# Order of the high-part and low-part products inside a weight unit of a two-block transformer kernel

## Chip, cores and metric

The kernel runs on one core of one Trainium2 chip. The metric is the device time of one execution in microseconds (us); a comparison is made by the median of several runs.

## Reference

Two transformer blocks over 256 tokens of width 2048 in float32. The first block has a mixer (a gated delta rule with eight heads beside a short convolution), an attention over 256 memory rows and a feed-forward layer with 5632 hidden features; the second has two kinds of causal attention with output gates. Nearly all arithmetic is products of 256 tokens with weight matrices:

```python
h = rmsnorm(x, mix_norm[l])
proj = h @ w_mix_in[l]
...
x = x + jnp.concatenate([y_gdn, y_sc], axis=-1) @ w_mix_out[l]
...
x = x + memory_xattn(h, mem_n, w_q[l], w_k[l], w_v[l], w_o[l])
x = x + conv_ffn(h, w_ffn_up[l], ffn_conv[l], w_ffn_down[l])
```

## Kernel before

**Products in parts.** Weights and operands are split into a high part (rounded to the float32r format that TensorE takes) and a low part, the exact remainder. A product is high times high, plus high weights times low operand, plus low weights times high operand. The moving operand of a K-tile, class `XT`, is one tile of 128 partitions by 512 columns: 256 columns of high part beside 256 of low part (`x.t`, with `x.hi` and `x.lo` its halves).

**Weight units.** The weights come in 704 units. A unit of `jobB` holds up to eight blocks of 128 x 128 weights for one tile of 128 output features, and a tile takes two units (three for some of `w_xo`). `blocks` (lines 207 to 224) issues a unit's products. Where `wide` is set, one matmul of 512 columns (line 217) multiplies the high weights with both halves of the operand, and one of 256 columns (line 222) the low weights with the high half. Otherwise there are two matmuls of 256 columns with the high weights (lines 219 and 220) and one with the low weights (line 222). The order is all high products of the unit, then all low products; in the last unit of a wide tile the last high product (line 224) comes at the very end, since it closes both halves of the bank. Every matmul has a weight load of its own. `jobA` (lines 306 to 308, 84 units) has the weights as moving operand and is not touched.

**Splitting and loading.** `stream` issues the work unit by unit. Ahead of unit i it issues `split_hi(i + 3)` (ScalarE copies the raw weights into a tile `whi`, line 352, four buffers) and `split_lo(i + 2)` (VectorE subtracts to make a tile `wlo`, line 359, three buffers), and the DMA load of a later unit through SyncE's queue, eight raw buffers deep. Then come the unit's products, and one step of every running piece of side work (norms, convolutions, softmax, the delta rule), whose instructions stand in the same queues of VectorE, ScalarE and GpSimd. Each engine runs its queue in the order in which it was written.

**Start.** `first_x` makes the first sixteen operand tiles: ScalarE the high part, VectorE the low part (line 537). In VectorE's queue the split of unit 0 stands behind operand tile 3, that of unit 1 behind tile 7, and those of the units from 2 on behind tile 15. The first three units belong to three different output tiles and all use operand tiles 0 to 7.

Of the kernel before, what the change touches and what calls it, by code (L numbers as in the profile page):

```python
# [15 lines left out]
PSUM = bass.MemoryType.PSUM  # L16
# [11 lines left out]
# columns of the packed per-partition parameters  # L28
# [11 lines left out]
# square constants: identity, ones, upper triangle, causal bias (negated), levels of the inverse,  # L40
# identities of 16 x 16 flattened
# [12 lines left out]
class XT(Ev):  # L54
    """One K-tile of a product's moving operand: [128, 256] as exact hi and lo parts."""
# [12 lines left out]
class Half:  # L68
    """[128, 256] float32 tiles, two to a slab."""
# [30 lines left out]
def block_rows(d):  # L100
    """Four 128 x 128 matrices in DRAM, spaced so that all their diagonal blocks lie evenly."""
    return bass.AP(tensor=d.tensor, offset=0, ap=[[P, P], [P * P + P, 4], [1, P]])
# [6 lines left out]
class Builder:  # L109
# [18 lines left out]
    # ---- storage  # L128
# [30 lines left out]
    # ---- side work: generators that go one step per weight unit  # L159
# [29 lines left out]
    # ---- the stream of weight units  # L189
# [17 lines left out]
    def blocks(self, ps, hi, lo, j0, xs, k0, n, first, last, wide):  # L207
        """128 x 128 blocks of weights, the high parts first. Wide: the high part's products with both
        parts of the operand lie side by side in the bank."""
        T, x = self.T, []  # L210
        c = [slice((j0 + j) * P, (j0 + j + 1) * P) for j in range(n)]
        end = n - 1 if wide and last else n
        for j in range(n):
            x.append(xs[k0 + j])
            self.need(x[j])
            if wide and j < end:
                T.matmul(ps, hi[:, c[j]], x[j].t, start=first and j == 0, stop=False)  # L217
            elif not wide:
                T.matmul(ps, hi[:, c[j]], x[j].hi, start=first and j == 0, stop=False)  # L219
                T.matmul(ps, hi[:, c[j]], x[j].lo, start=False, stop=False)  # L220
        for j in range(n):
            T.matmul(ps[:, 0:TOK], lo[:, c[j]], x[j].hi, start=False, stop=last and j == n - 1 and not wide)  # L222
        if end < n:
            T.matmul(ps, hi[:, c[end]], x[end].t, start=first and end == 0, stop=True)  # L224

    def merge(self, ps, out):
        """The two halves of a product's bank, added."""
        t = self.H("mg")
        self.AC.copy(t, ps[:, TOK:])  # L229
        yield  # L230
        self.V.tensor_tensor(out, ps[:, 0:TOK], t, ADD)
        self.rel()

    def times(self, ps, out, R):
        """A product's bank times a factor per token, once that is there. out: the tile, or a generator
        that gets it."""
        wide = ps.shape[1] > TOK
        if wide:
            t = self.H("ms")
            yield from self.merge(ps, t)  # L240
            while not R.ok:
                yield
            ps = t
        dst = out
        if not isinstance(out, bass.AP):
            dst = yield from out
        self.V.tensor_tensor(dst, ps, R.b, MUL)
        if not wide:
            self.rel()
        return dst  # L250

    def scaled_pre(self, ps, R):
        """The same into a tile with zeros before the first token."""
        pre = []

        def get():
            pre.append((yield from self.pre()))
            return pre[0][:, 4:]

        yield from self.times(ps, get(), R)  # L260
        return pre[0]

    def jobB(self, w, ui, parts, xs, post, ready=(), wide=False, srcs=None):
        """Features out on the partitions. parts: the K-tiles in each unit; post(ps) a generator."""
        st, units, k0 = {}, [], 0
        if wide:
            ready = ()
        K = sum(parts)
        for i, nk in enumerate(parts):
            def mm(hi, lo, k0=k0, nk=nk):  # L270
                if k0 == 0:
                    st["ps"] = self.mmbank()[:, 0 : (2 if wide else 1) * TOK]
                self.blocks(st["ps"], hi, lo, 0, xs, k0, nk, k0 == 0, k0 + nk == K, wide)

            last = i == len(parts) - 1
            pf = (lambda: [(ready, post(st["ps"]))]) if last else None
            src = self.A[w][ui + i] if srcs is None else srcs[i]
            units.append(self.unit(src, nk * P, mm, pf))
            k0 += nk
        return units  # L280

    def jobB_pair(self, w, ui, nk, xs, posts, ready=()):
        """Two column tiles in one unit."""
# [10 lines left out]
    def jobA(self, w, ui, K, xs, post, ready=(), early=None):  # L294
        """Tokens out on the partitions, 512 columns; two K-tiles to a unit. early(ps): the first half of
        the tokens is done first, and this follows it."""
# [32 lines left out]
    @staticmethod  # L329
    def skew(jobs, m):  # L330
        """The first units of the first m jobs before their second units."""
        out = []
        for i in range(max(len(j) for j in jobs[:m])):
            for j in jobs[:m]:
                if i < len(j):
                    out.append(j[i])
        for j in jobs[m:]:
            out += j
        return out
# [42 lines left out]
    # ---- small pieces  # L382
# [4 lines left out]
    def rsq(self, v, w):  # L387
        """v ** -0.5 for columns, with a Newton step."""
# [9 lines left out]
    def split_tile(self, src):  # L398
        """A slab's exact hi and lo parts."""
# [5 lines left out]
    def mm3(self, ps, a, b, first, last):  # L405
        """A product of two operands in hi and lo parts."""
# [4 lines left out]
    def sums(self, accs):  # L411
        """Column sums over the partitions of [128, 256] tiles, or of lists of them:
        [128 tokens, 2 for each]."""
# [12 lines left out]
    def spread(self, cols, n):  # L426
        """Columns [128 tokens, n] as rows over all partitions, in PSUM [128, n * 128]."""
# [12 lines left out]
    def g_rms(self, R, acc, width):  # L440
        """R: .c the factor per token [128, 2], .b the same over the partitions [128, 256]."""
# [13 lines left out]
    def prep(self, src, gain, x, acc, first):  # L455
        """The moving operand of a product after a norm whose factor per token comes later."""
# [11 lines left out]
    def conv(self, pre, taps, K):  # L468
        """Causal taps along the tokens; the tile holds 4 zeros before the first token."""
# [10 lines left out]
    # ---- constants and the first operand  # L480
# [22 lines left out]
    def first_x(self):  # L503
# [6 lines left out]
        # the tensor engine's clock is up to speed when the first operands are there  # L510
# [49 lines left out]
    # ---- mixer: decays and gates  # L560
    def softplus(self, z, w):
        """max(z, 0) + log1p(exp(-|z|)); the low part of 1 + y is carried along."""
# [97 lines left out]
    def g_gdn(self, g, t, done, base):  # L660
        """Four heads, 128 tokens: one chunk of the delta rule."""
# [213 lines left out]
    def g_base(self, base):  # L875
        """Inverses of the unit lower 16 x 16 diagonal blocks, one block to a partition."""
# [42 lines left out]
    # ---- mixer: short convolution  # L919
# [33 lines left out]
    # ---- memory  # L953
# [72 lines left out]
    # ---- residual stream  # L1026
# [14 lines left out]
    # ---- attention over the memory  # L1041
# [65 lines left out]
    # ---- feed-forward  # L1107
# [53 lines left out]
    def g_two_norms(self):  # L1161
        """The final norm of the first block and the first of the second."""
# [24 lines left out]
    def g_turn(self):  # L1187
        """The residual stream with the tokens on the partitions: 32 x 32 blocks turned by the vector
        engine, then put in their places on the way through DRAM."""
# [25 lines left out]
    # ---- second block: latents, rotary tables  # L1215
# [57 lines left out]
    def rope(self, r, out, rows):  # L1273
        """Rows in pairs of 32: x * cos + swapped x * sin, the sign in the sines."""
# [13 lines left out]
    def p_rf(self, ps):  # L1288
        """Rotary keys (rows 0-63) and forget gates (rows 64-71)."""
# [43 lines left out]
    # ---- causal attention of one head; keys 0-127 for the first queries, all for the others  # L1333
# [110 lines left out]
    def p_last(self, n):  # L1444
        """Tokens on the partitions: the last norm's factor is a column."""
# [20 lines left out]
    def g_out(self, ps, t):  # L1466
        """The last columns of half the tokens, the norm, the sum and the store."""
# [17 lines left out]
    def order(gd, zz, sc):  # L1485
        """The heads' tiles between others whose results take less work."""
        return gd[0:12] + zz[0:4] + sc[0:6] + gd[12:24] + zz[4:8] + sc[6:]

    # ---- the whole
    def build(self):  # L1490
# [12 lines left out]
        # streams are lists of units; hooks run before a unit's products  # L1503
# [5 lines left out]
        class Lazy(dict):  # L1509
            """K-tiles made by earlier work."""  # L1510
# [18 lines left out]
        # mixer  # L1529
# [4 lines left out]
        # tiles of w_mix_in: q 0-7, k 8-15, v 16-23, z 24-31, ba 32, then b, c, h of the convolution  # L1534
# [17 lines left out]
        # keys and values of the memory  # L1552
# [7 lines left out]
        # mixer out  # L1560
# [30 lines left out]
        # attention over the memory  # L1591
# [9 lines left out]
        for n in range(16):  # L1601
            # the last head's tiles in units of their own while it is still at work
# [6 lines left out]
        # feed-forward  # L1609
# [33 lines left out]
        # second block  # L1643
# [13 lines left out]
        # tiles of w_in_2: q_lat 0-5, kv_lat 6-9, rope and forget 10, gates of the first 11-18, fq 19-26,  # L1657
        # fk 27-34, gates of the second 35-42; fv apart
# [69 lines left out]
        # run  # L1728
# [25 lines left out]
# ---- host side: layout only  # L1754
# [4 lines left out]
def _b(w):  # L1759
    """[K, N] -> units of (up to 8 K-tiles) x 128 columns, K on the partitions."""  # L1760
# [8 lines left out]
def _a(w):  # L1769
    """[K, N] -> units of 2 K-tiles x 512 columns."""  # L1770
# [94 lines left out]
```

## Time and profile before

| what | value |
|---|---|
| median of 3 runs | 2087.55 us (2086.34 to 2087.66) |
| the profiled execution, first to last instruction | 2085.8 us |
| TensorE matmul busy, instructions | 2068.1 us (99%), 12526 |
| TensorE weight load busy, instructions | 1843.3 us (88%), 12526 |
| VectorE busy | 1463.8 us (70%) |
| ScalarE busy | 1081.7 us (52%) |
| DMA | 381.52 MB, mean 183 GB/s |

The profile has the span of the profiled execution; what lies around it in a run is 1.75 us by the median (2087.55 less 2085.8). Busy time of matmuls is the time in which at least one is under way; they overlap, so the length of one is more than its share, and the distance from one start to the next is what a product takes. PE stands for TensorE's matmuls, PEld for its weight loads, DVE for VectorE, ACT for ScalarE.

### The profile page before, as it was taken

To read this page: it belongs to the slowest core of one execution; us is meant where nothing else is said; L and a number is where in the kernel's file an instruction comes from. 1 tells how busy PE (TensorE), PEld (TensorE's weight loads), DVE (VectorE), ACT (ScalarE), POOL (GpSimd) and SP (SyncE) were. 2 spreads that over 40 slices of the span, in tenths; PEclk is the share of its full clock that TensorE was granted. 3 is DMA by queue.
4 is the path that set the end of the run, shared out by engine and by line. 5 is a ranking of instruction groups with operands and counts; after the bars stand their busy time and mean duration, and the time that the engine had idled before them with its cause. 6 is when DMAs were issued, how large, how long until landed. Compare 5 with 4: busy or idle time off the path is not lost.

```text
span 2085.8 us, 32625 instructions
## 1 busy us (share of the span) xinstructions
PE 2068.1 (99%) x12526; PEld 1843.3 (88%) x12526; DVE 1463.8 (70%) x2303; ACT 1081.7 (52%) x1701; POOL 186.7 (9%) x170
## 2 busy tenths in 40 slices
PE   8999999999999999999999999999999999999998
PEld 7999999988888898888888888888888889878886
DVE  7977668665467667688775778657779776557755
ACT  5654455544444555465543555435556644446653
POOL 3020012200001001100000000000009410000000
PEclk9999999999999999999999999999999999999999
DMA  7555446445565435555555555555546578444552
GB/s 279 172 163 183 152 142 225 162 162 191 193 228 187 161 118 190 191 189 188 186 194 182 192 192 188 186 192 188 186 152 220 200 220 222 161 143 152 196 186 102
DMA packets 136669, 381.52 MB, mean 183 GB/s; under 512 B 33601, under 2 KB 41537, under 8 KB 136513
## 3 DMA queue, kind: packets, MB, share of 16 engines
q1 hardware_dynamic: 136512, 379.44, 53.8%
q8 instruction: 98, 1.61, 0.3%
q14 instruction: 59, 0.48, 0.1%
HBM read 372.84 MB, written 5.90 MB: 182 GB/s over the span
## 4 chain that ended last, share of the span: by engine, by line
PE 98%; DVE 1%; DMA 0%; issue 0%; ACT 0%; SPq 0%; DVEq 0%
PE mm L217 42%; PE mm L222 28%; PE mm L219 5%; PE mm L220 5%; PE mm L306 4%; PE mm L308 4%; PE mm L307 4%; PE mm L224 3%; PE ps L1405 0%; PE ps L409 0%; PE ps L407 0%; PE ps L408 0%; PE ps L1404 0%; PE ps L781 0%; PE ps L764 0%; PE ps L1386 0%
## 5 line engine op out<-in xcount | busy, mean ns | idle before, releaser
L359 DVE TENSOR_TENSOR wlo<-raw,whi 128x1024 fp32r<-128x1024 f32 (+2 forms) x704 | 857.6, 1221 | 379.7 <-PE mm L222 133.6
L217 PE MATMUL mm<-x,whi 128*128 128x512 f32 x3786 | 965.1, 394 | 6.2 <-DVE x L537 5.7
L352 ACT CAST whi<-raw 128x1024 fp32r<-128x1024 f32 (+2 forms) x704 | 716.3, 1028 | 318.6 <-PE mm L308 106.6
L217 PEld LDWEIGHTS mm<-x,whi 128*128 128x128 f32 x3786 | 694.6, 189 | 138.1 <-DVE x L537 7.7
L222 PEld LDWEIGHTS mm<-x,wlo 128*128 128x128 f32 x4840 | 657.4, 191 | 41.4
L222 PE MATMUL mm<-x,wlo 128*128 128x256 f32 x4840 | 679.3, 283 | 0.0
L229 ACT COPY mg<-mm 128x256 f32<-128x256 f32 x182 | 67.8, 372 | 374.1 <-PE mm L224 373.9
L219 PE MATMUL mm<-x,whi 128*128 128x256 f32 x792 | 196.4, 285 | 0.0
L220 PE MATMUL mm<-x,whi 128*128 128x256 f32 x792 | 194.3, 283 | 0.0
L220 PEld LDWEIGHTS mm<-x,whi 128*128 128x128 f32 x792 | 151.5, 191 | 0.3
L219 PEld LDWEIGHTS mm<-x,whi 128*128 128x128 f32 x792 | 151.4, 191 | 0.2
L476 DVE SCALAR_TENSOR_TENSOR cv<-pre,cst,cv 128x256 f32<-128x256 f32 x264 | 130.5, 496 | 8.8 <-ACT cv L473 0.9
L306 PE MATMUL mm<-whi,x 128*128 128x512 f32 x336 | 131.9, 393 | 0.0
L308 PE MATMUL mm<-whi,x 128*128 128x512 f32 x336 | 130.9, 390 | 0.0
L307 PE MATMUL mm<-wlo,x 128*128 128x512 f32 x336 | 130.8, 389 | 0.0
L224 PE MATMUL mm<-x,whi 128*128 128x512 f32 x262 | 103.7, 396 | 0.0
L1154 POOL TENSOR_SCALAR hf<-hf,cst 128x256 f32<-128x256 f32 x16 | 25.2, 1575 | 684.3 <-PE mm L224 683.9
L308 PEld LDWEIGHTS mm<-whi,x 128*128 128x128 f32 x336 | 63.1, 188 | 13.3
L306 PEld LDWEIGHTS mm<-whi,x 128*128 128x128 f32 x336 | 63.1, 188 | 13.3 <-issue 0.7
L307 PEld LDWEIGHTS mm<-wlo,x 128*128 128x128 f32 x336 | 63.1, 188 | 12.9
L473 ACT ACTIVATE cv<-pre,cst 128x256 f32<-128x256 f32 x120 | 60.2, 505 | 0.0
L457 ACT ACTIVATE x<-hf,cst 128x256 fp32r<-128x256 f32 x32 | 16.3, 511 | 81.3 <-DVE hf L1031 81.3
(349 smaller groups left out, 1404.2 us busy)
## 6 DMA issues: line engine op xcount, KB each, us to landing
raw<-w_ffn_up SPq DMA_DIRECT2D x176, 512.0 KB, 3.2
raw<-w_mix_in SPq DMA_DIRECT2D x114, 512.0 KB, 3.9
raw<-w_in SPq DMA_DIRECT2D x86, 512.0 KB, 3.3
raw<-w_ffn_down SPq DMA_DIRECT2D x80, 512.0 KB, 3.2
raw<-w_xk SPq DMA_DIRECT2D x32, 512.0 KB, 3.3
raw<-w_xv SPq DMA_DIRECT2D x32, 512.0 KB, 3.2
raw<-w_mix_out SPq DMA_DIRECT2D x32, 512.0 KB, 3.2
raw<-w_xq SPq DMA_DIRECT2D x32, 512.0 KB, 3.3
```

Of the source, the lines that this page charges most:

```text
L217: T.matmul(ps, hi[:, c[j]], x[j].t, start=first and j == 0, stop=False)
L219: T.matmul(ps, hi[:, c[j]], x[j].hi, start=first and j == 0, stop=False)
L220: T.matmul(ps, hi[:, c[j]], x[j].lo, start=False, stop=False)
L222: T.matmul(ps[:, 0:TOK], lo[:, c[j]], x[j].hi, start=False, stop=last and j == n - 1 and not wide)
L224: T.matmul(ps, hi[:, c[end]], x[end].t, start=first and end == 0, stop=True)
L229: self.AC.copy(t, ps[:, TOK:])
L306: self.T.matmul(ps, x.hi[:, s], hi[:, c], start=k == 0, stop=False)
L307: self.T.matmul(ps, x.hi[:, s], lo[:, c], start=False, stop=False)
L308: self.T.matmul(ps, x.lo[:, s], hi[:, c], start=False, stop=k == K - 1)
L352: self.AC.copy(hi[:, 0:F], self.raw[i][:, 0:F])
L359: self.V.tensor_tensor(lo[:, 0:F], self.raw.pop(i)[:, 0:F], fl(self.whi[i][:, 0:F]), SUB)
L476: self.V.scalar_tensor_tensor(t, pre[:, o + j : o + j + TOK], taps[:, j : j + 1], t, MUL, ADD)
```

## The change

In `blocks` each high-part product is followed at once by the low-part product of the same block. For a wide unit the order is high 0, low 0, high 1, low 1 and so on; the last block of a tile has its low product first and its high product last. For other units it is the two high products and the low product of block 0, then those of block 1. The products, their operands and their number are the same. The remaining lines of the diff take out comments and docstrings.

```diff
     def blocks(self, ps, hi, lo, j0, xs, k0, n, first, last, wide):
...
         c = [slice((j0 + j) * P, (j0 + j + 1) * P) for j in range(n)]
-        end = n - 1 if wide and last else n
         for j in range(n):
             x.append(xs[k0 + j])
             self.need(x[j])
-            if wide and j < end:
-                T.matmul(ps, hi[:, c[j]], x[j].t, start=first and j == 0, stop=False)
-            elif not wide:
-                T.matmul(ps, hi[:, c[j]], x[j].hi, start=first and j == 0, stop=False)
+            begin, end = first and j == 0, last and j == n - 1
+            lo_part = lambda stop: T.matmul(ps[:, 0:TOK], lo[:, c[j]], x[j].hi, start=False, stop=stop)
+            if not wide:
+                T.matmul(ps, hi[:, c[j]], x[j].hi, start=begin, stop=False)
                 T.matmul(ps, hi[:, c[j]], x[j].lo, start=False, stop=False)
-        for j in range(n):
-            T.matmul(ps[:, 0:TOK], lo[:, c[j]], x[j].hi, start=False, stop=last and j == n - 1 and not wide)
-        if end < n:
-            T.matmul(ps, hi[:, c[end]], x[end].t, start=first and end == 0, stop=True)
+                lo_part(end)
+            elif end and not begin:
+                lo_part(False)
+                T.matmul(ps, hi[:, c[j]], x[j].t, start=False, stop=True)
+            else:
+                T.matmul(ps, hi[:, c[j]], x[j].t, start=begin, stop=False)
+                lo_part(False)
```

## Rows read from the trace of the kernel before

**Rows 1.** The page: shares of the last chain, then groups (count; busy us, mean ns).

```profile
PE 98%; DVE 1%; DMA 0%; issue 0%; ACT 0%; SPq 0%; DVEq 0%
...
L359 DVE TENSOR_TENSOR wlo<-raw,whi 128x1024 fp32r<-128x1024 f32 (+2 forms) x704 | 857.6, 1221 | 379.7 <-PE mm L222 133.6
L217 PE MATMUL mm<-x,whi 128*128 128x512 f32 x3786 | 965.1, 394 | 6.2 <-DVE x L537 5.7
...
L222 PE MATMUL mm<-x,wlo 128*128 128x256 f32 x4840 | 679.3, 283 | 0.0
...
L224 PE MATMUL mm<-x,whi 128*128 128x512 f32 x262 | 103.7, 396 | 0.0
```

**Rows 2.** Timeline of PE, one tile of two units: start us, us, instruction, count.

```profile
1004.20 2.00 PE L217 MATMUL mm<-x,whi 128*128 128x512 f32 x8
1006.03 1.11 PE L222 MATMUL mm<-x,wlo 128*128 128x256 f32 x8
...
1009.55 0.40 PE L224 MATMUL mm<-x,whi 128*128 128x512 f32 x1
1009.78 2.00 PE L217 MATMUL mm<-x,whi 128*128 128x512 f32 x8
```

**Rows 3.** Timeline of PE in narrow windows inside the run of nine from 1009.55.

```profile
1010.71 0.39 PE L217 MATMUL mm<-x,whi 128*128 128x512 f32 x1
...
1011.62 0.28 PE L222 MATMUL mm<-x,wlo 128*128 128x256 f32 x1
...
1011.73 0.40 PE L222 MATMUL mm<-x,wlo 128*128 128x256 f32 x2
```

**Rows 4.** Timeline of PE: one 512-column product between runs of 256.

```profile
41.39 0.40 PE L224 MATMUL mm<-x,whi 128*128 128x512 f32 x1
41.62 0.28 PE L219 MATMUL mm<-x,whi 128*128 128x256 f32 x1
41.74 0.28 PE L220 MATMUL mm<-x,whi 128*128 128x256 f32 x1
```

**Rows 5.** Timeline of PE: units with runs of six, then of four.

```profile
1749.58 0.40 PE L224 MATMUL mm<-x,whi 128*128 128x512 f32 x1
...
1751.68 0.40 PE L224 MATMUL mm<-x,whi 128*128 128x512 f32 x1
...
796.63 0.64 PE L222 MATMUL mm<-x,wlo 128*128 128x256 f32 x4
797.11 1.09 PE L217 MATMUL mm<-x,whi 128*128 128x512 f32 x4
798.04 0.40 PE L222 MATMUL mm<-x,wlo 128*128 128x256 f32 x2
```

**Rows 6.** Timelines of DVE and PE around the unit at 342.

```profile
342.83 1.22 DVE L359 TENSOR_TENSOR wlo<-raw,whi 128x1024 fp32r<-128x1024 f32 x1
...
342.09 0.28 PE L219 MATMUL mm<-x,whi 128*128 128x256 f32 x1
...
344.11 1.22 PE L222 MATMUL mm<-x,wlo 128*128 128x256 f32 x8
```

**Rows 7.** The same around the units at 163, 1567 and 71.

```profile
163.40 1.21 DVE L359 TENSOR_TENSOR wlo<-raw,whi 128x1024 fp32r<-128x1024 f32 x1
...
162.93 0.28 PE L219 MATMUL mm<-x,whi 128*128 128x256 f32 x1
...
1566.64 1.76 DVE L359 TENSOR_TENSOR wlo<-raw,whi 128x1024 fp32r<-128x1024 f32 x1
...
1567.07 2.00 PE L217 MATMUL mm<-x,whi 128*128 128x512 f32 x8
...
70.61 1.22 DVE L359 TENSOR_TENSOR wlo<-raw,whi 128x1024 fp32r<-128x1024 f32 x1
...
71.53 0.28 PE L219 MATMUL mm<-x,whi 128*128 128x256 f32 x1
```

**Rows 8.** The start: DVE and PE timelines, then a window (busy us and counts, granted clock).

```profile
23.71 1.21 DVE L359 TENSOR_TENSOR wlo<-raw,whi 128x1024 fp32r<-128x1024 f32 x1
...
23.97 2.00 PE L217 MATMUL mm<-x,whi 128*128 128x512 f32 x8
...
20.00:22.50 2.50, 2.50 (x7) 1.92 (x6) 2.50 (x5) 0.95 (x2) 1.84 (x2) 0.50 1.03 413
```

**Rows 9.** Timelines of DVE and PE in the feed-forward part.

```profile
1004.22 1.22 DVE L359 TENSOR_TENSOR wlo<-raw,whi 128x1024 fp32r<-128x1024 f32 x1 [1.34 <-PE mm L222]
...
1005.38 1.04 ACT L352 CAST whi<-raw 128x1024 fp32r<-128x1024 f32 x1
```

## Prediction

> **What bounds the kernel now.** I read the chain that ended last first: PE has 98% of it [rows 1], so the time is the sum of the distances from one matmul's start to the next, and an edit counts only if it changes such a distance or makes PE wait. The groups on the page come next. There are 3786 + 262 = 4048 wide products of 512 columns (lines 217 and 224), each with one low product of 256 columns; the other 792 of the 4840 low products belong to units that are not wide [rows 1]. The idle time ahead of line 217 is 6.2 us in all, and none stands ahead of line 222: PE today never waits for the low weights [rows 1]. The length printed for one matmul (394 and 283 ns) is no price, since they overlap. The price is in the timeline: two units, from 1004.20 to 1009.78, take 5.58 us for sixteen pairs of a wide and a low product, or 348.75 ns a pair [rows 2].
>
> Reading finer, the distance depends on the neighbours. Of the nine wide products from 1009.55 the first five take 1.16 us (232 ns each) [rows 2, 3] and the last four, from 1010.71 to 1011.62, take 0.91 us (227.5 each): a run of wide products settles to a lower price after some five [rows 3]. A run of eight low products takes 0.95 us (119 ns each) [rows 2], but the first one after a settled run of wide ones only 0.11 us [rows 3]. So a change of width has a price of its own.
>
> **The change part by part.** Nothing is added or removed: 12,526 matmuls with as many weight loads before and after, the same bytes, the same side work. Units that are not wide consist of 256-column products alone, at 0.12 us each in any order, so their order is worth nothing in itself. Two things do change.
>
> *First, when the low weights are wanted.* Until now a unit needs its `wlo` after eight wide products (1.83 us [rows 2]) or sixteen narrow ones (1.9 us); afterwards it needs it at its second or third product. In the usual stretch this costs nothing: VectorE's split at 1004.22 ends at 1005.44 for a unit that starts at 1009.78, over 4 us ahead [rows 2, 9]. But VectorE also has side work in its queue, and where that piles up the split finishes after its unit has begun, covered by the unit's high products. There the cover goes. I looked for units in which the split ends later than the start of the unit's second (wide) or third product:
> - at 342: the split ends at 342.83 + 1.22 = 344.05; the low weights are wanted at 342.09 + 0.24 = 342.33. Now the low products start at 344.11, just behind the split, so nothing is seen. Wait: 1.72 us [rows 6].
> - at 163: 163.40 + 1.21 = 164.61 against 162.93 + 0.24 = 163.17. Wait: 1.44 us, shared with the unit ahead of it [rows 7].
> - at 1567, where the residual's updates fill VectorE: 1566.64 + 1.76 = 1568.40 against 1567.07 + 0.23 = 1567.30. Wait: 1.10 us. Later units there are late by less, and this wait pays for them too [rows 7].
> - at 71: 70.61 + 1.22 = 71.83 against 71.53. Wait: 0.30 us [rows 7].
> - at the start: unit 2 begins at 23.97, its split ends at 23.71 + 1.21 = 24.92, wanted at 24.20. Wait: 0.72 us [rows 8]. That split stands behind all sixteen operand tiles in VectorE's queue, so what PE gains earlier, by low products in the gaps of unit 0, only makes it wait longer here.
>
> The sum is 5.28 us. A late PE delays what waits for PE (bank copies, the release of `wlo` buffers), but not the splits themselves, which are late from VectorE's own backlog. I take +5.3 us. If the waits overlap less or more, 3 to 7. At the start the granted clock is 0.50, the lower level of 1.2 GHz, until about 22.5 [rows 8]; a wait there could keep it low through another unit, up to 3 us more, which goes into the upper end alone.
>
> The high weights' buffers come free later, at the unit's end, not after its high products (about 0.95 us later, the length of the low run [rows 2]). A copy of 1.04 us made three units ahead [rows 9] hides that: a unit takes 2.79 us [rows 2], and the copy that ends at 1006.42 serves the unit behind the one that begins at 1009.78 [rows 2, 9]. I take 0; if the cover were gone in the few crowded units, under 1 us each. No DMA is issued in another order.
>
> *Second, the price of a pair.* The trace has no alternation, so I bound it. From below: the settled wide price and the best low price, 227.5 + 110 = 337.5 ns. From above: the unsettled wide price and the steady low price, 232 + 120 = 352. Nearest to the new order are shorter runs and the single wide product. Runs of six cost 2.10 us for six pairs, 350.0 ns; a run of four low and four wide costs 1.41 us, 352.5 ns; runs of eight 348.75 [rows 2, 5]. A single wide product between runs of 256 takes 0.23 us, and the narrow one behind it 0.12, not 0.11: 350 ns for the two, to about 5 ns [rows 4]. Shorter runs have so far been dearer, but a run of one cannot pay the whole settling over five. I take 350.5, between the single case and the runs of four and six. That is 1.75 ns above today, times 4048 pairs: +7.1 us. Each nanosecond in this is worth 4.0 us; it is the term that I know least.
>
> The sum against the span is 2085.8 + 5.3 + 7.1 = 2098.2 us; with the 1.75 us around the span it is 2099.95, so 2100.0 against a median of 2087.55.
>
> **The rivals.**
> - *Order is free.* Each product has a constant price, settled wide 227.5 and steady low 119, and only the transitions between runs cost today; if alternation is a steady state of its own, the pair is 346.5 ns. Then -2.25 x 4048 = -9.1 us, with the waits -3.8: 2083.7 us. For it: long runs do settle. Against it: the short runs and the single product do not [rows 4, 5].
> - *The low product hides in the wide one's slack* (the other side). Each low product comes at 110 ns, as the first behind a settled run does, and the wide ones stay at 227.5: 337.5 ns, -11.25 x 4048 = -45.5 us, with the waits 2047. For it: the 0.11 us row, which shows that a low product can be cheaper behind a wide one [rows 3]. Against it: behind a wide product that was not settled it is 0.12 [rows 4]. It decides as soon as a pair falls below 346.4 ns, where the gain passes the waits and 0.2% together.
> - *Never settled.* Every wide product costs 232 or more and each low one 120: 352 ns, +13.2 us, with the waits 2106, and to 2116 with 354.
> - *Only the waits.* A pair costs what it does now, because price depends on columns alone and what varies in a run is not tied to its order: 2087.55 + 5.3 = 2092.9. Against it: the distances repeat in the same places of a run [rows 2, 3]. The Trainium skill (TensorE: Matmul & The Clock Gate, section Back-to-back issue gap) prices an isolated matmul so, at columns by 2.4 plus 2.5 ns whatever stands beside it: an estimate of 325 ns a pair in either order, so no change but the waits. By that rule, the trace does not agree: 348.75 ns a pair, and a price that moves with the neighbours [rows 2, 3].
> - *Nothing is seen*: VectorE's backlog shifts so that the waits vanish, and pairs stay: 2087.5.
>
> **How the numbers follow.** A difference under 0.2% (4.2 us) is about what a measurement of this kernel can't tell from none. Forecast (2094 to 2106): 0.42. Never settled: 0.20. Order free: 0.18, of which a third below 2083.4 and the rest within 0.2%. Hidden low product: 0.08. Only waits: 0.08, half of it over 2091.7. Nothing: 0.04. Slower is 0.42 + 0.20 + 0.04 = 0.66; faster 0.08 + 0.06 = 0.14; the same 0.20. The range leaves out the hidden low product and the upper half of the case that never settles: 2081 to 2114, which takes in the order-free case and 3 us of clock at the start.
>
> **What the profile after would show.** The waits: idle time of PE or PEld ended by DVE's `wlo`, about 5 us in all and none today, at 71, 163, 342 and 1567. The pair: in a quiet stretch such as the one after 1004, sixteen pairs in 5.61 us for 350.5 ns (5.54 for order-free, 5.40 for the hidden low product, 5.63 for never settled). VectorE's and ScalarE's busy time should be the same to 1%. The prediction is wrong if alternation has a steady state that neither short runs nor the single product show, or if the splits, once PE waits for them, come earlier than the backlog suggests.

## The result and the profile after

The changed kernel takes 2109.67 us (median of 4 runs, 2106.23 to 2111.8) against 2087.61 us for the kernel before: the ratio is 1.0106, interval 1.0092 to 1.012, or 22.06 us slower. The profiled execution spans 2110.0 us, 24.2 us more than that of before; it is the slowest of the four. In the changed kernel line 225 is the wide product, 216 the low one, 223 the last wide one of a tile, 218 and 219 the two high products of other units, 361 and 354 the splits.

The page after, its chain and the groups that answer to [rows 1]:

```profile
PE 95%; DVE 3%; ACT 1%; issue 1%; DMA 0%; SPq 0%; DVEq 0%
...
L225 PE MATMUL mm<-x,whi 128*128 128x512 f32 x3786 | 1357.2, 400 | 2.2 <-ACT whi L354 1.5
L216 PE MATMUL mm<-x,wlo 128*128 128x256 f32 x4840 | 1321.5, 282 | 11.9 <-DVE wlo L361 11.8
L361 DVE TENSOR_TENSOR wlo<-raw,whi 128x1024 fp32r<-128x1024 f32 (+2 forms) x704 | 856.1, 1218 | 394.2 <-PE mm L216 141.6
```

Two things are to be seen. VectorE now has 3% of the chain, where it had 1%, and there is idle time ahead of the low products, 11.8 us of it ended by a low-weight split, where none stood before. Of these, 3.89 us lie ahead of the very first low product, at 13.43 in the start; they take the place of waits for operand tiles, which were 5.7 us in the kernel before [rows 1] and are 0.2 us now. And the counts are the same, as is VectorE's busy time in its split. Summed busy time of the matmul groups is of no use here: wide and low products now overlap each other, so each group seems to have grown by hundreds of us.

A quiet stretch, timeline of PE after, one row for each product now, to be held against the runs in [rows 2]:

```profile
1025.05 0.40 PE L225 MATMUL mm<-x,whi 128*128 128x512 f32 x1
1025.29 0.28 PE L216 MATMUL mm<-x,wlo 128*128 128x256 f32 x1
1025.41 0.40 PE L225 MATMUL mm<-x,whi 128*128 128x512 f32 x1
1025.65 0.28 PE L216 MATMUL mm<-x,wlo 128*128 128x256 f32 x1
1025.76 0.40 PE L225 MATMUL mm<-x,whi 128*128 128x512 f32 x1
1025.99 0.28 PE L216 MATMUL mm<-x,wlo 128*128 128x256 f32 x1
1026.11 0.40 PE L225 MATMUL mm<-x,whi 128*128 128x512 f32 x1
```

Three pairs take 1.06 us (1025.05 to 1026.11), 353.3 ns a pair, and the pattern of distances (0.24, 0.12, 0.24, 0.11, 0.23, 0.12) comes back after three. There is no idle time: PE loses this inside its own stream. Over a long stretch of the feed-forward part, the view of one line (duration ns min/median/max, first to last start) shows the last products of 71 tiles, before and then after:

```profile
L224 PE MATMUL mm<-x,whi x71: 396/396/396, 1104.5 to 1495.6; 128*128 128x512 f32 x71
```

```profile
L223 PE MATMUL mm<-x,whi x71: 395/400/400, 1103.1 to 1498.7; 128*128 128x512 f32 x71
```

Seventy tiles of sixteen pairs took 391.1 us and now take 395.6: 349.2 and 353.2 ns a pair, 4.0 ns more. But this price does not hold everywhere. In the same kernel, with the same alternation of widths, there are stretches that are cheaper (timeline of PE after):

```profile
400.54 0.40 PE L225 MATMUL mm<-x,whi 128*128 128x512 f32 x1
400.77 0.28 PE L216 MATMUL mm<-x,wlo 128*128 128x256 f32 x1
400.89 0.39 PE L225 MATMUL mm<-x,whi 128*128 128x512 f32 x1
...
405.39 0.40 PE L225 MATMUL mm<-x,whi 128*128 128x512 f32 x1
```

The fourteen pairs from 400.54 to 405.39 take 4.85 us, 346.4 ns a pair. Over the whole trace roughly one pair in ten of the alternating stretches runs at 346 to 348 ns, and most of the others at 352 to 354.

The waits, in the timelines of DVE and PE after, at the unit that began at 342.09 in [rows 6], and at the start, which answers to [rows 8]:

```profile
350.19 1.22 DVE L361 TENSOR_TENSOR wlo<-raw,whi 128x1024 fp32r<-128x1024 f32 x1
...
349.07 0.28 PE L218 MATMUL mm<-x,whi 128*128 128x256 f32 x1
349.19 0.28 PE L219 MATMUL mm<-x,whi 128*128 128x256 f32 x1
...
351.47 0.39 PE L216 MATMUL mm<-x,wlo 128*128 128x256 f32 x1 [2.00 <-DVE wlo L361]
...
25.28 1.21 DVE L361 TENSOR_TENSOR wlo<-raw,whi 128x1024 fp32r<-128x1024 f32 x1
...
26.55 0.58 PE L216 MATMUL mm<-x,wlo 128*128 128x256 f32 x1 [4.46 <-DVE wlo L361]
...
20.00:22.50 2.50, 2.08 (x12) 1.52 (x10) 2.50 (x5) 2.06 (x4) 1.50 (x1) 1.00 1.04 415
25.00:30.00 5.00, 3.45 (x11) 2.97 (x12) 4.84 (x4) 0.00 (x0) 3.01 (x3) 0.50 0.40 118
353.00:356.00 3.00, 3.00 (x16) 3.00 (x15) 1.71 (x3) 1.15 (x2) 1.65 (x1) 0.50 0.88 291
```

The two high products of block 0 are issued, and PE stands until the split ends at 351.41. At the start PE stands for 4.46 us. The last three rows are windows (busy time and count of PE, PEld, DVE, ACT and POOL, then clock, DMA share and GB/s). The granted clock was up, at 1.00, from 20 to 22.5, where it was 0.50 in the kernel before [rows 8]; behind the wait it is 0.50 from 25 to 30, the lower level, so the unit that had waited ran at half speed as well. Unit 3 begins at 31.41, and began at 26.77 in the kernel before: 4.6 us are lost by then. The same happens behind the 2.00 us wait at 351.47: the clock is 0.50 from 353 to 356. The unit that began at 348.05 in the kernel before begins at 358.56, and the delay grows there from 6.98 to 10.51 us; of these 3.5 us only 2.0 are the wait, and the rest is the slow clock behind it.

### The profile page after: what moved, and what is told of

It is laid out like the page before. It is cut to its first block, busy times and chain, and to the rows that moved or that the text cites. A ratio compares the mean times of both kernels' runs of the same rounds, so it can differ in the third digit from the quotient of the medians.

```text
span 2110.0 us, 32627 instructions
## 1 busy us (share of the span) xinstructions
PE 2084.4 (99%) x12526; PEld 1842.0 (87%) x12526; DVE 1463.3 (69%) x2303; ACT 1090.8 (52%) x1701; POOL 184.5 (9%) x170
## 4 chain that ended last, share of the span: by engine, by line
PE 95%; DVE 3%; ACT 1%; issue 1%; DMA 0%; SPq 0%; DVEq 0%
PE mm L225 42%; PE mm L216 26%; PE mm L218 4%; PE mm L219 4%; PE mm L308 4%; PE mm L310 4%; PE mm L309 4%; PE mm L223 3%; DVE wlo L361 1%; DVE x L539 0%; PE ps L1407 0%; DVE cv L478 0%; PE ps L410 0%; PE ps L411 0%; PE ps L409 0%
## 5 line engine op out<-in xcount | busy, mean ns | idle before, releaser
L225 PE MATMUL mm<-x,whi 128*128 128x512 f32 x3786 | 1357.2, 400 | 2.2 <-ACT whi L354 1.5
L216 PE MATMUL mm<-x,wlo 128*128 128x256 f32 x4840 | 1321.5, 282 | 11.9 <-DVE wlo L361 11.8
L361 DVE TENSOR_TENSOR wlo<-raw,whi 128x1024 fp32r<-128x1024 f32 (+2 forms) x704 | 856.1, 1218 | 394.2 <-PE mm L216 141.6
L216 PEld LDWEIGHTS mm<-x,wlo 128*128 128x128 f32 x4840 | 918.9, 190 | 38.4 <-DVE wlo L361 14.5
L225 PEld LDWEIGHTS mm<-x,whi 128*128 128x128 f32 x3786 | 713.5, 188 | 164.8 <-ACT whi L354 1.9
L218 PE MATMUL mm<-x,whi 128*128 128x256 f32 x792 | 226.8, 286 | 0.0
L219 PE MATMUL mm<-x,whi 128*128 128x256 f32 x792 | 224.7, 284 | 0.0
L219 PEld LDWEIGHTS mm<-x,whi 128*128 128x128 f32 x792 | 152.5, 193 | 0.3
L218 PEld LDWEIGHTS mm<-x,whi 128*128 128x128 f32 x792 | 152.5, 193 | 0.2
L223 PE MATMUL mm<-x,whi 128*128 128x512 f32 x262 | 104.5, 399 | 0.0
L308 PEld LDWEIGHTS mm<-whi,x 128*128 128x128 f32 x336 | 63.1, 188 | 13.3 <-issue 0.7
L233 DVE TENSOR_TENSOR ms<-mm,mg 128x256 f32<-128x256 f32 x140 | 58.5, 418 | 0.0
```

The lines of the kernel that those rows point to most:

```text
L216: lo_part = lambda stop: T.matmul(ps[:, 0:TOK], lo[:, c[j]], x[j].hi, start=False, stop=stop)
L218: T.matmul(ps, hi[:, c[j]], x[j].hi, start=begin, stop=False)
L223: T.matmul(ps, hi[:, c[j]], x[j].t, start=False, stop=True)
L225: T.matmul(ps, hi[:, c[j]], x[j].t, start=begin, stop=False)
L308: self.T.matmul(ps, x.hi[:, s], hi[:, c], start=k == 0, stop=False)
L361: self.V.tensor_tensor(lo[:, 0:F], self.raw.pop(i)[:, 0:F], fl(self.whi[i][:, 0:F]), SUB)
```

## Experiments

W is the theory that the loss is waits for the low weights, P that it is the price of changing width. The kernel before stood at a median of 2087.67 us in the first group and 2087.68 in the second.

**One low product early** (`e1_one_low`). Runs as before, but the first low product stands behind the first high one:

```diff
...
+            if j == 0:
+                T.matmul(ps[:, 0:TOK], lo[:, c[0]], x[0].hi, start=False, stop=False)
-        for j in range(n):
+        for j in range(1, n):
             T.matmul(ps[:, 0:TOK], lo[:, c[j]], x[j].hi, ...)
```

> Runs as before, but each unit's first low product stands right behind its first high product(s); the other seven stay at the end. Theory W (the loss is in waits for the low weights, which are wanted at the second or third product): the waits and the slow start of the changed kernel come back in full, about 8.6 us, so 2096. Theory P (the loss is in the price of changing from 512 to 256 columns at every product): only one more change of width in each of 506 wide units, at about 5 ns, so 2.5 us and 2090. Both theories at work: 8.6 + 2.5, about 2098 to 2099.

Measured 2102.19 us, 1.0067 (1.0055 to 1.008): 14.5 us, more than either theory or both gave. The waits are there; the view of waits of PE's weight loads (total, times, longest) in this kernel:

```profile
PEld mm L220 <- DVE wlo L359: 10.6, 8, 4.2
```

4.2 of these 10.6 us lie in the start, where the old order waits for operand tiles instead. The slow start of the changed kernel, which the expectation counted in, did not come back: the clock is 1.00 from 25 to 30,

```profile
25.00:30.00 5.00, 5.00 (x30) 4.41 (x29) 5.00 (x4) 1.06 (x1) 4.18 (x3) 1.00 0.86 246
```

and unit 3 begins at 27.01, only 0.2 us later than before. At 346.66 PE stands for 1.86 us, nearly as long as in the changed kernel, but the clock does not fall behind it (1.00 from 347 to 350), and the place costs 1.9 us instead of 3.5. The rest comes from the price: the 71 last products lie between these starts,

```profile
L224 PE MATMUL mm<-x,whi x71: 393/400/400, 1100.8 to 1495.0; 128*128 128x512 f32 x71
```

394.2 us for seventy tiles, 352.0 ns a pair. One low product inside a run of wide ones costs 2.8 x 8 = 22 ns, not the 5 I expected from the single wide product in [rows 4]. Times 506 units that would be 11 us if it held everywhere; it was read in this stretch alone. So this kernel says that both theories work, and that a lone change of width is dearer than I thought.

**Pairs, without the crowded units** (`e2_calm`).

```diff
+CROWDED = {i for a, b in ((0, 6), (16, 21), (44, 51), (92, 104), (250, 259), (524, 547)) for i in range(a, b)}
...
+        f = self.blocks_runs if self.cur in CROWDED else self.blocks_pairs
```

> Pairs as in the changed kernel, but the units of the crowded stretches (the first six, and those around 71, 163, 342, 815 and 1567 us; some 70 of 704) keep the old order, so that no low weights are wanted early there. Theory W: nothing is left, 2088. Theory P: 3.85 ns for each of about 3600 pairs, 13.9 us, so 2101 to 2102, with no wait for low weights in the trace over 0.3 us.

Measured 2100.16 us, 1.0057 (1.0044 to 1.0069): 12.5 us over before. PE waits for no low weights, and its weight loads wait for them once, for 0.3 us (PE's view of waits, all of it):

```profile
PE mm L222 <- DVE x L564: 5.1, 5, 2.9
PE ps L542 <- DVE zero L539: 1.5, 1, 1.5
PE mm L222 <- DVE x L1129: 0.5, 1, 0.5
PE mm L222 <- ACT whi L378: 0.4, 1, 0.4
```

With the two groups of wide products that the new order issues (3567 and 241), 3808 pairs cost 12.5 us, 3.3 ns each. That is less than the 4.0 ns of the long stretch, since the mean takes in the cheaper ones: the fourteen pairs at 400.54 of the changed kernel take 4.85 us here too (389.42 to 394.27). This is the price of the order without its waits; over 4048 pairs 13.3 us, and the other 8.8 of the 22.06 us are what the crowded units add, in waits and in the slow clock behind two of them.

**The first three units in the old order** (`e3_first3`).

```diff
+        f = self.blocks_runs if self.cur < 3 else self.blocks_pairs
```

> Pairs everywhere but in the first three units, which keep the old order. If the start with its 4.5 us wait and the unit at half clock is worth what the two traces show (4.6 us by the end of unit 2), then 2105; the spread of the changed kernel's runs (2106.2 to 2111.8) should shrink as well. If the start is only shifted and given back later, 2109.7.

Measured 2106.68 us, 1.0087 (1.0074 to 1.0101), runs from 2105.45 to 2107.89. That is 3.0 us under the changed kernel, and the spread falls from 5.6 to 2.4 us. The expectation was 4.6 us less, from the slowest of the changed kernel's runs. The intervals overlap, so the size is rough; the trace shows what is gone. Unit 2 runs at once, and the wait has moved to unit 3 and is short:

```profile
22.50 2.00 PE L221 MATMUL mm<-x,whi 128*128 128x512 f32 x8
24.42 1.21 PE L226 MATMUL mm<-x,wlo 128*128 128x256 f32 x8
25.47 0.40 PE L248 MATMUL mm<-x,whi 128*128 128x512 f32 x1
26.66 0.39 PE L239 MATMUL mm<-x,wlo 128*128 128x256 f32 x1 [0.79 <-DVE wlo L384]
...
25.00:30.00 5.00, 4.21 (x26) 3.48 (x25) 5.00 (x4) 1.08 (x3) 3.13 (x3) 1.00 0.72 220
```

The granted clock stays at 1.00 from 25 to 30, where it was 0.50. The wait at 342 is there as before (2.02 us at 346.65), and so is the fall of the clock behind it (0.50 from 348.5 to 351.5).

**Longer runs** (`e4_long_runs`). The other direction: a wide tile's last unit has its low products first, so they join those of the unit ahead, and its high products join those of the next tile.

```diff
+        if not (wide and last and not first):
+            return self.blocks_runs(...)
+        for j in range(n):
+            ...
+            T.matmul(ps[:, 0:TOK], lo[:, c[j]], x[j].hi, start=False, stop=False)
+        for j in range(n):
+            T.matmul(ps, hi[:, c[j]], x[j].t, start=False, stop=j == n - 1)
```

> The opposite direction: a wide tile's last unit has its low products first and its high products last, so that runs of one width are about sixteen long and changes of width are halved. Theory P: a pair of changes costs 17 to 20 ns in the trace of before, 253 fewer of them give -4.3 to -5 us, so 2082.5 to 2083.5. Theory W: the low weights are wanted at the start of every second unit, so waits as in the changed kernel where such a unit is late, none of the five great ones among them: 2087.6 to 2089.

Measured 2083.81 us, 0.9982 (0.9973 to 0.9991): 3.9 us faster than before, on P's side. Timeline of PE: sixteen of each width now stand together.

```profile
1002.90 1.98 PE L229 MATMUL mm<-x,whi 128*128 128x512 f32 x8
1004.72 1.12 PE L234 MATMUL mm<-x,wlo 128*128 128x256 f32 x8
1005.67 1.12 PE L215 MATMUL mm<-x,wlo 128*128 128x256 f32 x8
1006.63 2.00 PE L217 MATMUL mm<-x,whi 128*128 128x512 f32 x8
1008.47 1.98 PE L229 MATMUL mm<-x,whi 128*128 128x512 f32 x8
```

From 1002.90 to 1008.47 sixteen pairs take 5.57 us, 348.1 ns. What is short of the 4.3 to 5 us is a wait in the start: 1.03 us ahead of unit 3's low products at 27.56.

**Runs of two** (`e5_runs_of_two`).

```diff
...
+            high(j - 1, first and j == 1, False)
+            if not end:
+                high(j, False, False)
+            low(j - 1)
+            low(j)
+            if end:
+                high(j, False, True)
```

> Wide units in runs of two: two high products, then the two low ones (units that are not wide keep the old order). If each change of width has one fixed price (pairs: 353.3 ns against 346.7 for settled products, so 6.7 ns for a change there and back), runs of two cost 350 ns a pair, 3.6 us over before, and with waits of 2 to 4 us some 2094. If a run of wide products pays more the longer its settling lasts (runs of four paid 14 to 15 ns for a change there and back, runs of eight 17 to 20), runs of two pay 10 to 12 ns, 352 to 352.7 ns a pair, 12 to 15 us over before, and with the waits 2102 to 2106.

Measured 2091.0 us, 1.0017 (1.0008 to 1.0027), 3.3 us over before. The expectation from longer settling (2102 to 2106) is wrong. The one from a fixed price had the pair nearly right (350 ns) and its total, some 2094, too high by its waits. The view of its low products (all wide units) gives the pair:

```profile
L219 PE MATMUL mm<-x,wlo x1144: 274/279/286, 1099.8 to 1499.6; 128*128 128x256 f32 x191
```

1143 steps in 399.8 us are 349.8 ns a pair, 3.4 less than in runs of one. Outside the start PE waits for low weights only once, for 0.58 us at 1571.04, because units that are not wide keep the old order, and of the five great waits three were in such units. In the start it stands for 3.66 us at 13.43, in place of operand tiles, and for 1.86 us at 25.50; the clock does not fall there (1.00 from 25 to 30).

**All products of 512 columns** (`e6_all_wide_runs`, `e7_all_wide_pairs`). In wide units the low weights are multiplied by both halves of the operand, which adds a product of low parts that the kernel doesn't have; once in the order of before, once in pairs.

```diff
-            T.matmul(ps[:, 0:TOK], lo[:, c[j]], x[j].hi, ...)
+            T.matmul(ps if wide else ps[:, 0:TOK], lo[:, c[j]], x[j].t if wide else x[j].hi, ...)
```

> The order of before, but in wide tiles the low weights are multiplied by both halves of the operand, so that every matmul of a wide unit has 512 columns (it adds a product of two low parts that is not in the kernel before). With no change of width each product should cost the settled 227 ns: 454 ns a pair, 105 ns more than now for 4048 pairs, so about 2085.8 + 425 = 2511 for the span.

> The same products of 512 columns in the order of the changed kernel. If the price of pairs lies in the change of width: 454 ns a pair as in the runs, and a time within the waits of that kernel (0 to 9 us more, since slower units leave the splits more time). If it lies in going to and fro between the tiles of high and low weights: some 4 ns a pair more in a quiet stretch, 16 us.

One run each: 2510.92 and 2514.32 us. The last products of a tile lie, in runs and in pairs, at

```profile
L224 PE MATMUL mm<-x,whi x55: 389/390/390, 1104.3 to 1496.0; 128*128 128x512 f32 x55
```

```profile
L223 PE MATMUL mm<-x,whi x56: 389/390/390, 1100.4 to 1499.4; 128*128 128x512 f32 x56
```

54 tiles in 391.7 us and 55 in 399.0: 453.4 ns a pair in both. Going to and fro between high and low weights costs nothing while the width stays; 226.7 ns a product in either order. With the width constant the part of the bank that is written stays the same as well, so these runs do not tell a change of columns from a change of that part. PE waits for low weights in pairs only (8.2 us, of which 5.45 in the start in place of operand tiles); that this makes the 3.4 us between the two single runs is likely and not shown.

**Longer runs with the old start** (`e8_long_runs_start`). As `e4_long_runs`, with the first six units in the old order.

```diff
-        if not (wide and last and not first):
+        if self.cur < 6 or not (wide and last and not first):
```

> The long runs again, with the first six units in the old order, since the trace of the long runs shows 0.9 us lost there to a wait for the low weights. If that wait was a loss of its own: 2083.0 (0.9 less than 2083.81); if the start is made up for elsewhere: 2083.8.

Measured 2082.64 us, 0.9977 (0.9968 to 0.9986), 5.0 us faster than before. Against the kernel without this edit it is 1.2 us by the medians, in another group of runs and with overlapping intervals, so that part is likely and not shown. In its trace the wait in the start is gone, but two others, of 0.61 us at 164.98 and 0.57 us at 344.91, have come in. It is the fastest version measured, on both sides of the change.

## Why the prediction was right, and where its terms were not

The direction and the range were right: slower, 2109.67 in 2081 to 2114. The likeliest case, 2100.0 with 2094 to 2106, was too low by 9.7 us; the time lies in what the prediction called the case that never settles (2106 to 2116; by the prediction's own terms 354 ns gives 2114, not 2116). Both steps of the sum were real, and both were too small: 12.4 us were forecast and 22.1 measured, so the range held by its width and not by its middle.

**The waits** were to be 5.3 us, and 8.8 are left when the pairs are paid. The places are those foreseen, and outside the start their sizes were about right: at 71, 163, 342 and 1567 the working gave 0.30, 1.44, 1.72 and 1.10 us, and the trace has PE idle there for 0.23, 0.63, 2.00 and 0.54 (idle time is counted from a product's modelled end, so the delay is a little longer). What failed is the start, and the clock. At the start the working said 0.72, because it took the split's old end and let PE arrive later; 4.6 us were lost there in the profiled execution. The low products in the gaps of unit 0 brought PE to unit 1 at 18.56 and not 19.66. Unit 1 then ran at the upper level of the clock (0.98 from 18 to 22.5), which in the kernel before it did not have up to 22.5 [rows 8], so that PE was at unit 2 at 21.68 and not 23.97. The split came 1.57 us later than in the execution before (25.28 against 23.71), part of which is VectorE's own: the instruction ahead of the split took 1.23 us and not 0.16. So PE stood for 4.46 us, and the clock fell. The prediction had the clock at the start in its upper end alone, as a level that stays low; in fact it had risen and fell again. That the clock could fall behind a wait in the middle of the kernel was in no term; at 351 it did, for some 1.5 us. The first three units are worth some 3 us by the medians (`e3_first3`).

**The price of a pair** was to be 350.5 ns, 1.75 above before. It is 353.2 in the quiet stretch, and the whole gives 3.3 ns above before (`e2_calm`), so this term was 13.3 us and not 7.1. It is no single price either: 346 to 348 ns in some stretches and 352 to 354 in most, where the prediction took one figure for all 4048 pairs. The step that failed is the choice between the bounds: I stood closest to the single wide product [rows 4], a reading good to 5 ns, and to the shorter runs. The upper bound of 352, five unsettled wide products with a steady low one [rows 2, 3], was itself passed by a little: in the pattern of three pairs a wide product costs 0.23 to 0.24 us.

**The rivals.** That order is free is out as a forecast of the whole: with the width constant it is free (453.4 ns in both orders), with the width changing it cost 3.3 ns a pair. But the steady state that this rival assumed, 346.5 ns a pair, exists: the fourteen pairs from 400.54 run at 346.4. So a change of width goes with the loss and does not always bring it. The Trainium skill (TensorE: Matmul & The Clock Gate, section Back-to-back issue gap) gives a price by columns alone for an isolated matmul. Taken for a stream, it would leave no room for neighbours; the runs here don't agree, at 348.1, 349.2, 349.8 and 353.2 ns a pair for runs of sixteen, eight, two and one. That a low product hides behind a wide one is half true: the low products come at 0.11 to 0.12, but the wide ones pay more than that back.

**The cover of the high weights.** The prediction took 0 for their later release, and that held: the one wait of PE that a high split ends, 1.5 us, is at the very first product, before any buffer is used a second time.

What stays open is why a wide product is dearer near a change of width, and what decides whether a stretch of pairs runs at 346 or at 353 ns. The traces show the sizes, and that in long runs the higher price dies out over five products; with the width constant the weights' tile has no part in it. No run here looks inside.

## What to carry to other kernels

Where TensorE's stream has no gaps, the order of products is still worth a look: put those of one width together, across units where the buffers allow (here 0.9982 of the time with runs of sixteen), and measure the pair for each length of run, since counting the changes of width does not give its price. An order that interleaves two operands also moves the moment at which the second one is wanted; look for the units where it is ready just in time today, since there the cover is in the old order. A wait may cost twice when the clock falls behind it, as behind the 4.46 us in the start and the 2.00 us at 351; behind 1.86 us in two other runs it did not fall, so look at the clock's windows and not at the waits alone.

## What was not expected of the hardware

A change of width there and back has no fixed price. Against settled products (226.7 ns for 512 columns, 120 for 256, so 346.7 a pair) it costs 21 ns in runs of sixteen or eight (1.4 x 16 = 22 by 348.1; 2.5 x 8 = 20 by 349.2), 22 ns for one low product alone in a run of wide ones, and only 6 to 7 in runs of two or one (3.1 x 2; 6.5). So in this stretch runs of two are nearly as good as runs of eight, and runs of one are the worst of all that were tried. And runs of one have two prices: where the pair takes 346.4 ns, as from 400.54, the change costs nothing.
